# Queries and keys of a recurrence by seven products, and the first two products of every pair of blocks inside the recurrence

## The chip, the cores and the metric

The kernel runs on one core of a Trainium2 chip. The metric is the time of one execution on the device in microseconds (us); lower is better. The core has a matrix engine (TensorE, PE in the profile), a vector engine (VectorE, DVE), an engine for activation functions (ScalarE, ACT), a general one (GpSimd, POOL) and one that issues most of the transfers (SyncE, SP). Each works through its own queue in order and waits for the others by semaphores. TensorE writes to eight banks (PSUM), from which DVE and ACT read.

## The reference, cut to what matters

One layer of an encoder over x (1024 tokens x 1024 features, float32). The input projection is one matrix product; its columns are cut into the parts that the kernel treats one by one:

```python
proj = x @ w_in[l]
(aq, ak, av, gq, gk, gv, gout, lr_f, lr_b, gate_a, gate_g) = jnp.split(proj, IN_SPLITS, axis=-1)
...
# dilated windowed attention on aq, ak, av: 12 heads in 3 groups, mixed to 4 heads x 64
...
la_f = log_sigmoid(lr_f @ w_lr_fwd + b_lr_fwd) / TAU      # decays, low rank 16; la_b likewise
o_gla = forward scan(gq, gk, gv, la_f) + backward scan(gq, gk, gv, la_b)   # 4 heads, chunks
o_gla = o_gla * lax.rsqrt(jnp.mean(jnp.square(o_gla), axis=-1, keepdims=True) + NORM_EPS)
y_gla = o_gla * gla_norm_g * silu(gout)
...
merged = sigmoid(gate_a) * (y_attn @ w_attn_branch) + sigmoid(gate_g) * (y_gla @ w_gla_branch)
x = layernorm(ALPHA * x + merged @ w_out)
ff = square(relu(x @ w_ff1 + b_ff1)) @ w_ff2 + b_ff2
x = layernorm(ALPHA * x + ff)
```

gq and gk are 256 columns each (4 heads x 64), gv 512, gout 512, the two gates 1024 each, aq, ak and av 768 each.

## The kernel before, in words

**Three matmuls for one.** Every float32 operand is split into a rounded part (hi) and the rest (lo), by `halve` (a copy on ACT, a subtraction on DVE, lines 153 and 154) or `load_w` (93 and 95). `mm3` (lines 102 to 104) then does hi x hi, hi x lo and lo x hi. So one product over a slice of 128 features is three matmuls. A block is 128 columns of the projection; its result is kept feature by token, 128 x 1024.

**Seven products for eight.** Two blocks together are a pair. Weights (128-column blocks, halves of K) and x (halves of K, halves of the tokens) form a 2 x 2 by 2 x 2 block product, which `proj` does with seven products instead of eight (Strassen and Winograd's form). Each product is 12 matmuls of 512 columns. x's blocks are B11, B12 (first half of K; first and second half of the tokens), B21 and B22; its sums are T1 = B12 - B11, T3 = B22 - B12, T2 = B22 - T1 and T4 = B21 - T2. The weights' sides are A11, A12, A22 and sums S1 to S4, made by `side` from raw weights. The products: m1 = A11 B11, m2 = A12 B21 (these two together are the plain result of block 0 on the first half of the tokens), m6 = S2 T2, m7 = S3 T3, m5 = S1 T1, m4 = A22 T4, m3 = S4 B22. A step is one product with, three steps ahead, the making of its side (`steps`).

**The stages.**

1. Start (lines 180 to 206): x comes in slice by slice; the first blocks of queries and keys (blocks 0 and 2) are multiplied plainly, four banks, 96 matmuls. Constants and the bias rows follow.
2. `gla_v_units(0)`: eight units of 24 matmuls of 272 columns make low-rank rows and the first 240 columns of values. Values stay in the tile `gv`, queries and keys in tiles `q0` ... `k3`. The low-rank rows are transposed (`lrt`, lines 319 to 325).
3. The recurrence (`gla_head`, four heads). A head runs `pre1` (decays: the matmul `zp`, exponentials, logarithm, two scans on DVE), `pre2` (factors; keys are multiplied by `ex`, queries by `zb`), `turn` (transposes of keys), `intra`, `kv`, `states`, `out` and `outt`. Its steps depend on one another, so between them stand fills: eight units of values, four units that multiply blocks 1 and 3 plainly (24 matmuls each), and 14 fills of two halves each: the first two products (m1, m2) of the ten pairs in `KEPT`, and a part of the attention's values. Two units come before head 0's `pre1`, six between its `pre2` and its `turn`. `step` ties what it wraps to the last matmul issued, so TensorE runs this stage strictly in the order written.
4. x's sums (`xsum`, line 530, from x loaded once more) are made at the recurrence's end: T1 beside head 3, T3, T2 and T4 behind it.
5. `proj` for 16 pairs (`todo`): two of the swish gate, six of attention queries and keys, eight of the merge gates. Ten need five products only, the others seven. Between steps stand the attention's 24 tiles, eight per group: `visit` (scores, softmax, transposes, values) at set distances, 2 steps, then 1.75, and for the last nine visits what is left of the steps, 25 steps over nine visits. The last group's tiles also mix the three groups (lines 931 to 940, 955 to 971) and send weights through DRAM (`spread`, `loadw`). `silu` multiplies the recurrence's result by the swish gate and stores it.
6. `branches` loads both mixers' results and halves them; then the merge, the output projection and the MLP.

The order on each engine is set when the program is built: what is ready first by a planner's reckoning goes first, in order of the text, unless `issue_after` ties it behind a given instruction on the same engine. Pools are stacks at both ends of the memory; a pool with `reuse_waits="tile"` lets each of its tiles wait only for those tiles whose memory it takes. In a pool tiles lie in the order of their first mention.

Of the kernel before, what the change touches and what calls it, by code (L numbers as in the profile page):

```python
# [72 lines left out]
def build(tc, io):  # L73
# [32 lines left out]
    def mmtile(w=512):  # L106
# [4 lines left out]
    ygdr = dr.tile([4, 128, S], F32, name="ygdr")  # L111
# [9 lines left out]
    upk = dr.tile([10, 128, 512], F32, name="upk")  # L121
# [5 lines left out]
    XQ = {f"B{i + 1}{j + 1}": xp.tile([128, 2, 4, 512], F32R, tag="act", name=f"x{i}{j}")  # L127
          for i in range(2) for j in range(2)}
# [8 lines left out]
    def xl(k, sl):  # L137
        return xpart(1, k, sl)

    tbp = P.open("tbl", side="right")  # L140


    stp = P.open("start")
    w0 = {nm: (wp.tile([128, KT, 128], F32R, tag="whi", bufs=4, name="whi"),
               wp.tile([128, KT, 128], F32R, tag="wlo", bufs=4, name="wlo")) for nm in "qk"}

    def fetch(src, shape, tag, bufs, eng=SP):
        raw = stp.tile(shape, F32, tag=tag, bufs=bufs, name=tag)
        eng.dma_start(raw, src)
        return raw  # L150
# [4 lines left out]

    def start_w(k, n):
        if k:
            raw = fetch(io["wqk"][:, k:k + n], [128, n, 2, 128], f"w{n}", n)
        for i, nm in enumerate("qk"):
            hi, lo = w0[nm]  # L160
            r = raw[:, :, i] if k else fetch(io["wqk"][:, 0:1, i], [128, 1, 128], "w0", 2)
            halve(hi[:, k:k + n], lo[:, k:k + n], r, None if k else V.tensor_copy)

    def start_x(k, hf=None):

        sl = slice(0, S) if hf is None else slice(hf * 512, hf * 512 + 512)
        first = (k, hf) == (0, 0)
        raw = fetch(io["xT"][k * 128:(k + 1) * 128, sl], [128, S if hf is None else 512],
                    "xr" if hf is None else "xrh", 5 if hf is None else 4, A if first else SP)
        for j in range(2) if hf is None else (hf,):  # L170
            js = slice(j * 512, j * 512 + 512)
            r, h = raw[:, js] if hf is None else raw, xh(k, js)
            if first:
                V.tensor_copy(h[:, 256:512], r[:, 256:512])
                A.copy(h[:, 0:256], r[:, 0:256])
                V.tensor_tensor(xl(k, js), r, h.bitcast(F32), op=OP.subtract)
            else:
                halve(h, xl(k, js), r)


    zt = stp.tile([128, 512], BF16, name="zt")
    V.memset(zt, 0.0)
    zp = avp.tile([128, 512], F32, tag="av", name="zp")
    for _ in range(7):
        T.matmul(zp, zt[:, 0:128], zt, start=True, stop=True)

    ps0 = {("q", 0): mmtile(), ("q", 1): mmtile(), ("k", 0): mmtile(),
           ("k", 1): scp.tile([128, 512], F32, tag="sc", name="sc")}
    for k in range(KT):
        n = {0: 1, 1: 1, 2: 2, 4: 2, 6: 2}.get(k)  # L190
        if k == 0:
            start_x(0, 0)
        if n:
            start_w(k, n)
        if k == 0:
            start_x(0, 1)
        elif k < 3:
            start_x(k, 0)
            start_x(k, 1)
        else:  # L200
            start_x(k)
        for nm, hf in (("q", 0), ("k", 0), ("q", 1), ("k", 1)):
            hi, lo = w0[nm]
            sl = slice(hf * 512, hf * 512 + 512)
            mm3(ps0[nm, hf], [(hi[:, k], lo[:, k], xh(k, sl), xl(k, sl))],
                first=k == 0, last=k == KT - 1)


    ident = cp.tile([128, 128], F32, name="ident")
    SP.dma_start(ident, io["c_ident"])  # L210
    sgt = cp.tile([128, 128], F32, name="sgt")
    SP.dma_start(sgt, io["c_sgt"])
    cols = cp.tile([128, 56], F32, name="cols")
    SP.dma_start(cols, io["cols"])
    mhalf = cp.tile([128, 8], F32, name="mhalf")
    V.memset(mhalf, -0.5)

    rb = tbp.tile([99, 12], F32, name="rb")
    SP.dma_start(rb, io["rb"])
    oh = tbp.tile([99, 512], F32, name="oh")  # L220
    SP.dma_start(oh, io["c_oh"])
    tp = trp.tile([128, 512], F32, tag="tr", name="tr")
    T.matmul(tp[0:12], rb, oh, start=True, stop=True)
    tsb = tbp.tile([12, 512], F32, name="tsb")

    V.tensor_scalar(tsb, tp[0:12], 8.0, None, op0=OP.mult)
    SP.dma_start(trow, tsb)
    P.close("start")
    P.close("tbl")
    stg = P.open("stg", bufs=2, side="right")  # L230
    tmp = P.open("tmp", side="right")
    xr_t, xb_t = ring(tmp, [128, S], F32, 4, "xraw"), ring(tmp, [128, 512], F32, 3, "xb22")

    kp4 = P.open("keep", reuse_waits="tile")

    def piece4(name, dtype=F32, shape=(128, S), parts=128):
        return kp4.tile([parts, *shape[1:]], dtype, tag="k4", bufs=10, name=name)

    gp = P.open("gla", reuse_waits="tile")
    lr = gp.tile([128, 8, 3, 32], F32, name="lr")
    wz = gp.tile([96, 4, 128], F32, name="wz")

# [72 lines left out]
    for u in gv_units[1]:  # L317
        u()
# [1668 lines left out]
```

## Time and profile before

| what | value |
|---|---|
| median of 3 runs | 1362.0 us (1361.73 to 1362.38) |
| profiled execution, its own time | 1362.74 us |
| its span, from the first to the last instruction | 1360.9 us |
| mean granted TensorE clock | 0.998 |
| start until the last of the first 96 matmuls | to 29.9 us |
| values' first eight units and the recurrence | about 30 to 220 us |
| projections with attention | about 220 to 579 us |
| merge, output projection, MLP | from 579 us |

Rows of the profile are read so. A row of the timeline is start, duration, engine, line, operation, output <- inputs, shape, and how many; in square brackets stands how long the engine had been idle and what it waited for. A row of a window is its bounds and length, then for PE, PEld (weight loads), DVE, ACT and POOL the busy time and the number of instructions, then the granted clock, the transfers' share and GB/s. A row of groups is line, engine, operation, shapes and count, then busy time and mean ns of one, then idle time before them. A row of waits is who waited for whom: us in total, times, longest.

### The profile page before, as it was taken

The numbers are of one execution on the slowest core, as the hardware profiler recorded it, in microseconds if no ns is written. First come the engines' busy times: TensorE is split into PE (matmuls) and PEld (weight loads), VectorE is DVE, ScalarE is ACT, GpSimd is POOL, SyncE is SP. The second block draws the span as 40 slices with busy tenths as digits, with TensorE's granted clock in tenths as the row PEclk, the third lists the DMA queues.
The fourth block names the chain that finished last, engine by engine and source line by source line (L and its number), as shares of the span: only waits on it lengthen the run. The fifth ranks groups of instructions, "written<-read, shape, count | busy, mean of one in ns | idle before, by whom it ended". The sixth has DMA issues, their size and how long they took to land.

```text
span 1360.9 us, 18993 instructions
## 1 busy us (share of the span) xinstructions
PE 1349.8 (99%) x6781; PEld 1121.9 (82%) x6781; DVE 1025.2 (75%) x1764; ACT 630.9 (46%) x1199; POOL 122.6 (9%) x193
## 2 busy tenths in 40 slices
PE   9999999999999999999999999999999999999998
PEld 7988898898777777788888888888888888888886
DVE  6377669778776788767677777887767997786987
ACT  5346656323344444454337545555556433333343
POOL 0000001111443432000000000000000000000001
PEclk9999999999999999999999999999999999999999
DMA  7315754777656677666836466666736955444313
GB/s 250 81 46 177 246 170 144 263 256 220 187 193 217 175 212 198 201 200 235 291 143 230 139 216 201 226 200 203 267 149 193 364 193 165 145 154 155 93 32 124
DMA packets 126306, 256.96 MB, mean 189 GB/s; under 512 B 36053, under 2 KB 45877, under 8 KB 126212
## 3 DMA queue, kind: packets, MB, share of 16 engines
q1 hardware_dynamic: 117044, 229.55, 51.2%
q0 software_dynamic: 8736, 25.77, 6.2%
q8 instruction: 53, 0.87, 0.3%
q10 hardware_dynamic: 432, 0.44, 0.1%
q14 instruction: 41, 0.34, 0.1%
HBM read 175.61 MB, written 81.14 MB: 189 GB/s over the span
## 4 chain that ended last, share of the span: by engine, by line
PE 92%; DMA 3%; DVE 2%; ACT 2%; SPq 1%; issue 1%; ACTq 0%; DVEq 0%
PE ps L102 18%; PE ps L103 18%; PE ps L104 18%; PE mm L102 9%; PE mm L104 9%; PE mm L103 9%; PE avp L910 1%; PE sc L871 1%; PE tr L895 1%; DMA xrh<-in_xT 1%; ACT xr L1378 1%; PE sc L104 1%; PE sc L102 1%; PE sc L103 1%; DMA pwhi<-in_wtv 0%
## 5 line engine op out<-in xcount | busy, mean ns | idle before, releaser
L1359 ACT CAST T<-hp 128x1024 fp32r<-128x1024 f32 x36 | 37.9, 1052 | 109.0 <-PE ps L103 69.5
L103 PE MATMUL ps<-B,B 128*128 128x512 f32 x160 | 62.2, 389 | 0.0
L104 PE MATMUL ps<-B,B 128*128 128x512 f32 x160 | 62.2, 389 | 0.0
L1865 POOL TENSOR_TENSOR mv<-mv,mhalf 128x1 f32<-128x1 f32 x8 | 7.0, 881 | 607.3 <-DVE mv L1864 605.8
L102 PE MATMUL ps<-B,B 128*128 128x512 f32 x160 | 60.9, 390 | 0.5 <-ACT B L1359 0.5
L883 ACT ACTIVATE e<-e,sm 128x256 f32<-128x256 f32 (+2 forms) x96 | 43.3, 453 | 37.2 <-DVE sm L877 29.6
L102 PE MATMUL ps<-T,T 128*128 128x512 f32 x144 | 56.0, 389 | 0.0
L103 PE MATMUL ps<-T,T 128*128 128x512 f32 x144 | 56.0, 389 | 0.0
L104 PE MATMUL ps<-T,T 128*128 128x512 f32 x144 | 56.0, 389 | 0.0
L102 PE MATMUL ps<-B,T 128*128 128x512 f32 x144 | 56.0, 389 | 0.0
L103 PE MATMUL ps<-B,T 128*128 128x512 f32 x144 | 56.0, 389 | 0.0
L104 PE MATMUL ps<-B,T 128*128 128x512 f32 x144 | 56.0, 389 | 0.0
L1760 DVE TENSOR_TENSOR acc<-ps,acc 128x512 f32<-128x512 f32 x68 | 45.6, 685 | 12.7 <-PE ps L104 12.2
L1360 DVE TENSOR_TENSOR T<-hp,T 128x1024 fp32r<-128x1024 f32 x36 | 43.9, 1221 | 14.8 <-ACT T L1359 14.7
L102 PE MATMUL mm<-x,whi 128*128 128x512 f32 x136 | 53.4, 404 | 1.0 <-ACT x L153 0.6
L103 PE MATMUL mm<-x,whi 128*128 128x512 f32 x136 | 53.7, 395 | 0.0
L104 PE MATMUL mm<-x,wlo 128*128 128x512 f32 x136 | 53.5, 395 | 0.0
L102 PE MATMUL ps<-T,fraw 128*128 128x512 f32 x128 | 49.6, 390 | 0.4 <-ACT T L1359 0.4
L103 PE MATMUL ps<-T,fraw 128*128 128x512 f32 x128 | 49.8, 389 | 0.0
L104 PE MATMUL ps<-T,fraw 128*128 128x512 f32 x128 | 49.6, 389 | 0.0
L633 DVE TENSOR_TENSOR cr<-cu,mm 128x512 f32<-128x512 f32 x44 | 35.2, 799 | 19.2 <-PE mm L104 18.8
L1478 ACT ACTIVATE c<-c,cols 128x512 f32<-128x512 f32 x48 | 34.7, 725 | 30.2 <-DVE c L1539 13.7
(595 smaller groups left out, 4279.9 us busy)
## 6 DMA issues: line engine op xcount, KB each, us to landing
hdr<-c SPq DMA_DIRECT2D x112, 256.0 KB
hp<-hdr SPq DMA_DIRECT2D x56, 512.0 KB
spill<-cr SPq DMA_DIRECT2D x54, 256.0 KB
praw<-in_wfm SPq DMA_DIRECT2D x16, 512.0 KB
pwhi<-in_wfm SPq DMA_DIRECT2D x16, 512.0 KB
gate<-spill SPq DMA_DIRECT2D x32, 256.0 KB
wa<-in_w SPq DMA_DIRECT2D x16, 512.0 KB
wb<-in_w SPq DMA_DIRECT2D x16, 512.0 KB
```

The costliest lines, as they stand in the source:

```text
L102: T.matmul(ps, lh, rh, start=first and i == 0, stop=False, skip_group_check=more)
L103: T.matmul(ps, lh, rl, start=False, stop=False, skip_group_check=more)
L104: issued["pe"] = T.matmul(ps, ll, rh, start=False, stop=last and i == n - 1, skip_group_check=more)
L633: issued["add"] = V.tensor_tensor(o, a, b, op=OP.add)
L871: mm = T.matmul(sps[i][:, pr, 0:w], q[ps_, pr], k[ps_, pr, 0:w], start=True, stop=True)
L883: issued["exp"] = A.activation(e, e, AF.Exp, bias=sm[:, h:h + 1], scale=-1.0, accum_out=sm[:, 4 + h:5 + h])
L895: T.transpose(tp[0:hi - lo, pr, j], b["e"][i][:, pr, lo:hi], ident)
L910: return T.matmul(av[64 * i:64 * i + 64, pr], vv[:, h * 64:h * 64 + 64], b["et"][i][p0:p0 + vv.shape[0], pr, j], start=j == pr == 0, stop= ...
L1359: A.copy(o[:, 0], src)
L1360: V.tensor_tensor(o[:, 1], src, o[:, 0].bitcast(F32), op=OP.subtract)
L1478: A.activation(q, src, AF.Relu, bias=cols[:, 2 * j + f:2 * j + f + 1])
L1760: V.tensor_tensor(m, p, m, op=OP.add)
```

## The change

- **The start** holds x's first half of tokens only. Per slice of K it multiplies the query blocks 0 and 1 (m1 and m2 of two pairs: block 0 with 2, and 1 with 3), with a copy of m1 after four slices, and the first four value units' first group. Then come value units and, beside them, x's second half and the sums T1, T3, T2; T4 is written over B12, after B21 has been loaded again. B22 and T4 are stored to DRAM (`xsd`).
- **Queries and keys** of both pairs then take the other five products each (`psteps`). Results go to DRAM (`spill`) and come back as `q`, `k` per head (`load_qk`); values go through DRAM too (`gvd`) into `gv`. Head 0's `pre1` stands behind the first of the ten products, its `pre2` and `turn` behind the last.
- **Fills** are 20 in place of 26: m1 and m2 of all 16 pairs and the four values parts. No units of values, queries or keys are left there.
- **Projections** then need five products for each of the 16 pairs; T4 and B22 come back from DRAM. There are 90 steps instead of 98; the last nine visits share 19 steps.
- `silu` halves its result into the tiles of B11 and B21 instead of storing it; `branches` only loads the attention's result, into T3's tile. Tiles and pools are laid out anew (`pa`, `tk`, `xr`, `tp2`).
- All products of `proj` are now tied behind the last matmul; before, only from step 10 on.

The core of the diff:

```diff
-            with behind("pe" if "fixed" in issued else "none"), behind("small"):
+            with behind("pe"), behind("small"):
...
+    for k in range(KT):
+        start_x(k, 0)
...
+        for i in range(2):
+            o = first_sides[2 * (k // 4) + i]
+            with behind("pe"):
+                mm3(pq[i], [(o[:, 0, ks], o[:, 1, ks], xh(k, h0), xl(k, h0))], k == 0, k in (3, 7), k > 3)
+        for t in range(4):
+            v_unit(t, 0, pv[t], (k,))
...
+    for t in range(4):
+        v_unit(t, 1, v_bank(t))
...
+    for k in range(4):
+        b11, b12, b22 = block(k, 0), block(k, 1), block(k + 4, 1)
+        sub(b11, b12, b11)
+        split_x("T1", k, b11)
...
+    for t in range(4, 8):
+        v_unit(t, 0, v_bank(t))
+    lp = [trp.tile([128, 512], F32, tag="tr", name="tr") for _ in range(2)]
+    for t in range(8):
+        with behind("pe"):
+            mm = T.transpose(lp[t // 4][0:96, t % 4 * 128:t % 4 * 128 + 128], lr[:, t].rearrange("p a b -> p (a b)"), ident)
...
+    for t in range(4, 8):
+        v_unit(t, 1, scp.tile([128, 272], F32, tag="sc", name="sc"))
...
+    SP.dma_start(xsd[0], XQ["B22"].bitcast(F32))
+    for k in range(4):
+        b21, b22 = block(k, 1), block(k + 4, 1)
+        sub(b22, b21, b22)
+        split_x("T4", k, b22)
+    for prep, _ in psteps[4:]:
+        prep()
...
+    P.close("xr")
+    kp4 = P.open("keep", reuse_waits="tile")
...
+    def load_qk(h):
+        b, i = h // 2, h % 2
+        for nm, base in (("q", 0), ("k", 2)):
+            qk[nm, h] = t = piece4(f"{nm}{h}")
+            for d in range(2):
+                after_raw(SP.dma_start, t[64 * d:64 * d + 64], spill[base + b, 64 * i:64 * i + 64])
...
-            ex = piece4("ex")
+            ex = gp.tile([128, S], F32, tag="ex", name="ex")
...
-    fill(2)
-    step(heads[0]["pre1"])
-    heads[0]["pre2"]()
-    fill(6)
+    for n, (_, do) in enumerate(psteps):
+        if n == 1:
+            step(heads[0]["pre1"])
+        for f in do:
+            f()
+        if n == 4:
+            issued["raw"] = issued["sp"]
+            for h in range(2):
+                load_qk(h)
...
+    SP.dma_start(xsd[1], XQ["T4"].bitcast(F32))
+    P.close("pa")
+    gp = P.open("gla", reuse_waits="tile")
+    heads[0]["pre2"]()
+    firsts[1][1]()
+    gv = gp.tile([128, 8, 512], F32, name="gv")
+    for i in range(2):
+        after_raw(SP.dma_start, gv[:, 4 * i:4 * i + 4], gvd[512 * i:512 * i + 512].rearrange("(t p) f -> p t f", p=128))
...
+    tp2 = P.open("tp2", reuse_waits="tile")
+    for i, nm in ((1, "T4"), (0, "B22")):
+        XQ[nm] = tp2.tile([128, 2, 4, 512], F32R, name=f"y{nm}")
+        after_raw(SP.dma_start, XQ[nm].bitcast(F32), xsd[i])
...
-                          i - 2 if 1 < i < 2 + KEPT else None))
+        projs.append(proj(bl, r, (lambda i=i: projs[i + 2]["raw"]()) if 1 < i < NP - 2 else None, banks_of[i > 1], i))
...
-    n1 = len(steps) - 7
+    n1 = len(steps) - 5
...
-    for i in range(8):
-        for n, f in zip((6 + 2 * i, 12 + 2 * i), silu(i // 2, i % 2)):
+        for n, f in zip((10 + 2 * i, 16 + 2 * i), silu(i // 2, i % 2)):
```

Pool `pa` holds, in this order, B22, B12 (later T4), `first_sides`, `lr`, `rb`, two copies of m1 and the staging ring `fcr`; `keep` holds eight slots of 4 KB (`k4`: `lrt`, `wz`, `q`, `k`, `zb`, `L`), `wzr` and a mask; `gla` begins with `sm`, `ex` and `gv`.

864 lines of the change are left out of this document (404 added, 460 removed).

## The prediction

> **What bounds the kernel now.** I read the page's busy times and its chain of waits first, then TensorE's waits, then its timeline for the time from one matmul's start to the next.
>
> ```profile
> span 1360.9 us, 18993 instructions
> PE 1349.8 (99%) x6781; PEld 1121.9 (82%) x6781; DVE 1025.2 (75%) x1764; ACT 630.9 (46%) x1199; POOL 122.6 (9%) x193
> ...
> PE 92%; DMA 3%; DVE 2%; ACT 2%; SPq 1%; issue 1%; ACTq 0%; DVEq 0%
> ...
> PE tr L102 <- DVE cr L633: 0.8, 1, 0.8
> PE sc L977 <- DVE sm L877: 0.7, 2, 0.5
> ```
>
> TensorE (PE) is the bound: 99% busy, 92% of the chain, and the longest waits inside the kernel are under a microsecond. So the change is worth the matmuls it removes less the holes it opens in PE's queue.
>
> A busy matmul reads 389 ns because matmuls overlap; what one costs is the distance between starts:
>
> ```profile
> 473.05 0.39 PE L104 MATMUL mm<-xT,pwlo 128*128 128x512 f32 x1
> ...
> 476.45 0.39 PE L104 MATMUL mm<-x,px 128*128 128x512 f32 x1
> ...
> 53.35 0.29 PE L102 MATMUL mm<-whi,x 128*128 128x272 f32 x1
> 53.73 0.29 PE L102 MATMUL mm<-whi,x 128*128 128x272 f32 x1
> ```
>
> Between the first two rows lie 15 steps: 3.40/15 = 0.2267 us for 512 columns, so a product (12 matmuls) takes 2.72 us and a fill of two halves 5.44. The last two are three matmuls apart: 0.127 us for 272 columns, 3.03 us for a unit of 24.
>
> **Term 1, the matmuls removed.** Before, blocks 0 to 3 (queries and keys) cost 4 blocks x 2 halves x 24 = 192 matmuls. After, two pairs of blocks cost 7 products x 12 each: 168. 24 x 0.2267 = **-5.44 us**. The other six pairs' first two products only move into the recurrence, 144 matmuls or 32.6 us; values, gates and attention keep their counts.
>
> **Term 2, the start.**
>
> ```profile
> 4.26 1.19 PE L102 MATMUL mm<-x,whi 128*128 128x512 f32 x2
> 5.67 0.63 PE L104 MATMUL mm<-x,wlo 128*128 128x512 f32 x1
> 6.10 0.63 PE L103 MATMUL mm<-x,whi 128*128 128x512 f32 x1
> ...
> 14.65 0.50 PE L102 MATMUL mm<-x,whi 128*128 128x512 f32 x1 [0.58 <-ACT x L153]
> 25.16 1.03 PE L223 MATMUL tr<-oh,rb 99*12 99x512 f32 x2
> 29.67 0.39 PE L104 MATMUL sc<-x,wlo 128*128 128x512 f32 x1
> 0.00:20.00 20.00, 18.24 (x65) 12.65 (x66) 12.44 (x27) 11.85 (x23) 1.73 (x9) 1.00 0.82 289
> ```
>
> From 4.26 to 29.9 us PE ran 96 matmuls (21.8 us) and the bias rows (1.0): 2.9 us lost, partly to spacings of 0.43 us at first, partly waiting for x. After, one slice of K brings half as much x (256 KB), 128 KB of weights and 139 KB of value weights, and holds 6 x 0.2267 + 12 x 0.127 = 2.9 us of work: 523 KB per 2.9 us is 180 GB/s, against the 289 GB/s of the window row. Only six of the 512-column matmuls fall into the slow beginning (6 x 0.2 = 1.2 us lost, not waiting on x). I take **-1.45**, bounds 0 and -2.9.
>
> **Term 3, transposes of the low-rank rows.** They now stand in strict order behind value unit 7, whose copy by VectorE (DVE) the last one needs; before, a later unit covered it. Seven transposes run meanwhile. **+0.4**, bounds 0 and 1.
>
> **Term 4, the decays' first matmul.** Call F the end of the last value unit. PE reaches head 0's first matmul (`zp`, in `pre1`) at F + 0.5 (bias rows) + 2.72 = F + 3.2, the second at F + 3.45. Everything on PE is queued behind it. It needs `lrt` and `wzr`, whose memory in `keep` is the closed pool `xr`'s: the x blocks from which T4 is made, and pair 1's raw weights. T4 is written over B12, whose first slice of K the last value unit reads until F - 2.65 (7 of its 8 slices, 0.38 each, are left); ScalarE's first copy takes 0.6 more. So from about F - 1.9 DVE has 4 halves of T4, A22, S4, the bias rows, `wzr` (2) and `lrt` (4):
>
> ```profile
> 224.69 0.69 DVE L691 TENSOR_TENSOR praw<-praw 128x512 f32<-128x512 f32 x1
> 225.30 0.69 DVE L530 TENSOR_TENSOR xraw<-xraw 128x512 f32<-128x512 f32 x1
> 225.90 0.69 DVE L154 TENSOR_TENSOR pwhi<-psum,pwhi 128x512 fp32r<-128x512 f32 x1
> L306 DVE CAST wzr<-wz 96x512 fp32r<-96x512 f32 x1 | 0.4, 423 | 0.4 <-DMA wz<-in_wz 0.4
> ```
>
> Starts are 0.60 apart, so 12 x 0.60 + 0.4 = 7.6 us, done at F + 5.7: **+2.3**. Bounds: 0.5 if `lrt` goes first; 4.5 if the load of `wz` gets the slot of the bias table and starts only behind its matmul. Before, the same work lay among value units.
>
> **Term 5, head 0's keys.** The new code goes from the last product of queries and keys (end E) straight to `turn(0)` through `step`; before, six value units lay between. `turn` needs keys x `ex`, and `ex` now lies in pool `gla`. Tile sizes: const to `keep` end at byte 164,800 of a partition; `sm` takes 192, so `ex` is 164,992 to 169,088. `pa` is 62,528 long and, with the layout before ending at 229,344, begins at 166,816 with B22. B22 is read by that very last product (m3). So ScalarE's exponential cannot start before E:
>
> ```profile
> 73.96 1.06 ACT L360 ACTIVATE ex<-zb 128x1024 f32<-128x1024 f32 x1
> 75.05 1.22 DVE L361 TENSOR_TENSOR k<-k,ex 128x1024 f32<-128x1024 f32 x1 [1.58 <-ACT ex L360]
> ...
> 79.66 1.03 PE L371 MATMUL tr<-ident,k 128*128 128x128 f32 x8
> 80.63 1.16 PE L411 MATMUL sc<-q,k 64*128 64x128 f32 x16
> L364 DVE TENSOR_TENSOR q<-q,zb 128x1024 f32<-128x1024 f32 x4 | 4.9, 1231 | 2.0 <-ACT zb L363 1.9
> ```
>
> The last matmul's tail is 0.39 - 0.23 = 0.16; + 1.06 + 1.22 and some 0.1 for hand-overs = 2.6; then 0.2 before `intra`, whose queries are multiplied 1.2 later while the transposes take 1.03: **+2.8**. Upper bound 5.9, if `ex` must also wait for the last store from `fcr` (0.6 addition and a landing of 2.6, row below). Lower bound 2.6. `gv` is loaded over B22 and T4, so 2 x 1 MB start at E too: at 289 GB/s the second half lands at E + 7.3 + 2.6 = 9.9; `kv(1)` comes at E + 2.8 + 1.0 + 1.2 + 5.4 + 0.9 = 11.3. **+0.2**, upper bound 2.4 at the page's mean of 189 GB/s.
>
> **Term 6, the last attention tiles.** The last nine visits were spread over 25 products, now over 19: two products per visit instead of 2.78. Before shows one such visit, between these rows:
>
> ```profile
> 503.02 0.42 DVE L877 CUSTOM_DVE_ANT_0 e<-sc,strip 128x256 f32<-128x256 f32 x1
> ...
> 511.70 0.42 DVE L877 CUSTOM_DVE_ANT_0 e<-sc,strip 128x256 f32<-128x256 f32 x1 [0.81 <-PE sc L871]
> ...
> 503.85 0.28 PE L977 MATMUL sc<-ident,f 128*12 128x128 f32 x1 [0.45 <-DVE sm L877]
> 512.53 0.27 PE L977 MATMUL sc<-ident,f 128*12 128x128 f32 x1
> ```
>
> 8.68 us, of which DVE waited 0.81 for the scores; four of DVE's operations belonged to products. A pair whose first two products are kept needs 14 operations (5 halvings, 4 sums, 5 additions) for 5 products, 5.6 per visit: 1.6 x 0.60 = 0.96 more. That uses up the 0.81 and leaves 0.15; eight visits: 1.2, and a little for the spread's wait (0.45 above): **+1.5**. Bounds: 0 (sides are made three products ahead) and 8 x 0.96 = 7.7 (the wait stays).
>
> **Term 7, before the merge.**
>
> ```profile
> L1141 SPq DMA_DIRECT2D pre<-yadr x4: 319/342/382, 563.0 to 568.0; - x4
> DMA to landing us min/median/max: 2.2/2.6/4.7
> ...
> 561.09 0.42 DVE L940 TENSOR_TENSOR mixed<-W 128x256 f32<-128x256 f32 x1
> ...
> L102 PE MATMUL ps<-ya,whi x32: 389/389/389, 578.9 to 632.6; 128*128 128x512 f32 x32
> ```
>
> From the last mixing to the merge there were 17.8 us; five products instead of seven leave 12.4. Store, load, two landings of 2.6 and the halvings need about 9: **+0.3**, bounds 0 and 3.
>
> **At nothing.** Block sums T1 to T3 on DVE and ScalarE lie beside 12 value units, 36 us; DVE needs some 27 there (24 operations for the sums, 8 for x, 7 for sides at 0.60, weights and low-rank rows 3.6), so 9 are to spare. B22 and T4 come back as 4 MB, 14.5 us at 289 GB/s, beside the last fills and six products (16 us) that don't use them; uncovered, they would cost those 14.5. The extra stores and loads (SP issues) sit in queues nobody on PE waits for but `gv`'s. Six splits of 1024 columns join the recurrence, but 32 operations on block sums leave it, and twelve halvings (A11, A12) leave the attention. The swish gate's eight halvings move up from before the merge to steps 16 to 30 (4.8 us), where the fullest stretch was
>
> ```profile
> 300.00:320.00 20.00, 19.97 (x88) 16.22 (x87) 16.84 (x24) 5.33 (x9) 2.91 (x5) 1.00 0.68 211
> ```
>
> DVE at 16.84 of 20 us, with PE hardly waiting: they fit in what is left over some 40 us.
>
> Sum: -5.44 - 1.45 + 0.4 + 2.3 + 2.8 + 0.2 + 1.5 + 0.3 = **+0.6**. The profiled execution took 1362.74 (span 1360.9), the median is 1362.0; so 1363.3 for such an execution, **1362.6** as a median. About 0.2%, 2.7 us, is what a measurement of this kernel can tell from no change.
>
> **Rivals.** *Cover holds*: DVE takes `lrt` early and the attention's backlog is absorbed; only terms 1, 2, 3 and 5 stand: -3.7, 1358.3. For it: no TensorE wait over 0.8 us before; against: those waits had units between.
>
> *DVE becomes the bound of the last visits* (slower): its wait for the scores stays in the queue's order, and each of eight visits grows by 0.96. It decides once a visit's DVE work passes 8.7 us. 7.7 in place of 1.5: 1368.8.
>
> *The clock falls after the hole of term 5.* In the tail, where PE waits much, the granted clock drops:
>
> ```profile
> 1352.00:1354.00 2.00, 2.00 (x3) 0.67 (x2) 1.93 (x7) 0.57 (x1) 0.62 (x1) 0.51 0.00 0
> ```
>
> Holes of 0.8 us left no such mark. If it comes, the price is that of the beginning: half speed from the first dummy matmul (1.2 us) to 7.3, 6.1 us, half of it lost: 3.0, so 1365.6.
> The Trainium skill (TensorE: Matmul & The Clock Gate, Part 1: The HAM clock gate) has PE fall to half rate after about one idle window of 3.4 us, and Part 4 does not count transposes as busy; by it hole and transposes, 3.8 us, would be enough, at an estimated 1.7 us. No row here shows a hole of that size.
>
> **Chances.** Forecast (within 0.2%) 0.40; cover holds 0.30, all faster; DVE bound 0.14; clock 0.10; a worse hole in term 4 or 5 (to 1365.7) 0.06. So faster 0.30, same 0.40, slower 0.30. Range 1357.0 to 1370.0: below it lies only a start with nothing lost, above it bounds that add up. The forecast's own range is 1359.3 to 1364.7.
>
> **What would show it.** PE waiting on ScalarE or DVE 2 to 4 us ahead of L371's successor (first transposes of keys), and 1 to 4 us ahead of the first `zp`; `ex`'s first exponential starting right behind the last product; DVE over 9.5 tenths in the last visits. No hole at the first transposes would refute term 5; PE waits there together above 8 us would make it slower.

## The result and the profile after

The changed kernel takes 1411.27 us in the median of four runs (1409.84 to 1413.13), the kernel before 1361.87 (1361.05 to 1362.38): a ratio of 1.0364, with a 95% interval of 1.0346 to 1.0382. The sum of the prediction said +0.6 us and 1362.6; the medians say +49.4. The profiled executions differ by 47.1 in span, and the rest of this text explains those 47.1.

First the page of the kernel after, its span and TensorE's busy time:

```profile
span 1408.0 us, 19086 instructions
...
PE 1355.5 (96%) x6757; PEld 1124.3 (80%) x6757; DVE 1032.8 (73%) x1778; ACT 632.9 (45%) x1199; POOL 117.8 (8%) x185
```

PE has 24 matmuls fewer (6781 before), as term 1 counted. Yet it is busy for 5.7 us more (1349.8 before) and idle for 41.4 more: 1408.0 - 1355.5 = 52.5, before 11.1. Were all matmuls as fast as before, PE would be busy for 5.4 less; so about 11.1 us went into matmuls that ran slowly. 41.4 - 5.4 + 11.1 = 47.1: two questions, then, why PE waits and why it is slow.

Who PE waited for (line waiting, line waited for, us in total, times, longest):

```profile
PE sc L964 <- DVE f L958: 12.6, 4, 6.7
PE tr L523 <- DVE k L513: 10.6, 1, 10.6
PE sc L488 <- DVE wzr L459: 7.2, 1, 7.2
PE mm L102 <- ACT pwlo L149: 4.5, 1, 4.5
PE mm L102 <- DVE fcr L153: 4.2, 1, 4.2
PE mm L102 <- ACT fcr L367: 2.2, 1, 2.2
PE sc L964 <- DVE sm L864: 1.6, 2, 0.9
```

These seven groups make 42.9 us, where before no wait inside the kernel passed 0.8. By windows (bounds, length, PE's busy time first, the granted clock third from the end) they lie in few places:

```profile
72.00:140.00 68.00, 45.85 (x195) 36.42 (x194) 30.06 (x38) 18.66 (x26) 0.48 (x3) 0.82 0.56 179
140.00:270.00 130.00, 130.00 (x769) 112.65 (x768) 85.21 (x117) 77.98 (x179) 10.41 (x16) 1.00 0.65 207
270.00:300.00 30.00, 25.05 (x112) 20.80 (x111) 14.47 (x22) 9.81 (x16) 0.00 (x0) 0.94 0.48 169
520.00:640.00 120.00, 105.60 (x599) 82.89 (x596) 87.32 (x271) 43.90 (x116) 27.56 (x43) 0.96 0.68 200
```

The ten products of queries and keys and head 0's first steps (72 to 140) lose 22 us in waits, the projections' start 5, the last attention visits 14; the recurrence itself loses nothing. For the start, head 0 and the projections' beginning the order of time reads as follows (start, duration, engine, line; in brackets how long the engine stood idle, and for whom; SPq is SP's queue of transfers):

```profile
31.05 0.39 PE L102 MATMUL mm<-whi,xB 128*128 128x272 f32 x1 [2.23 <-ACT fcr L367]
...
70.13 0.32 SPq L705 DMA_DIRECT2D xsd<-xB  x1
71.92 0.31 SPq L444 DMA_DIRECT2D trow<-xr  x1
77.11 0.33 SPq L457 DMA_DIRECT2D wz<-in_wz  x1
79.95 0.68 DVE L459 TENSOR_TENSOR wzr<-wz,wzr 32x512 fp32r<-32x512 f32 x1
80.78 1.19 PE L488 MATMUL sc<-lrt,wzr 96*128 96x512 f32 x2 [7.25 <-DVE wzr L459]
82.20 0.63 PE L103 MATMUL mm<-xT,fs 128*128 128x512 f32 x1
82.63 0.63 PE L104 MATMUL mm<-xT,fs 128*128 128x512 f32 x1
...
86.34 1.23 DVE L495 TENSOR_TENSOR zb<-zb,L 128x1024 f32<-128x1024 f32 x1 [2.62 <-ACT L L492]
87.67 2.28 DVE L497 TENSOR_TENSOR_SCAN L<-rmask,zb 64x1024 f32<-64x1024 bf16 x1
89.99 2.29 DVE L498 TENSOR_TENSOR_SCAN L<-rmask,zb 64x1024 f32<-64x1024 bf16 x1
92.31 0.69 DVE L153 TENSOR_TENSOR fcr<-fu,mm 128x512 f32<-128x512 f32 x1
93.05 0.80 PE L102 MATMUL mm<-xB,fs 128*128 128x512 f32 x1 [4.19 <-DVE fcr L153]
...
119.09 1.04 ACT L93 CAST whi<-raw 128x1024 fp32r<-128x1024 f32 x1 [9.55 <-DMA raw<-in_wfm]
123.72 1.06 ACT L512 ACTIVATE ex<-zb 128x1024 f32<-128x1024 f32 x1
126.09 1.97 PE L523 MATMUL tr<-ident,k 128*128 128x128 f32 x8 [10.55 <-DVE k L513]
...
278.65 0.50 PE L102 MATMUL mm<-xT,pwlo 128*128 128x512 f32 x1 [4.54 <-ACT pwlo L149]
```

In each case an engine that isn't the bound stands in its own order: something late is ahead of something that PE needs.

- At 31.05 the second value units want a bank whose copy (L367, at 30.42) stands on ACT behind casts of x.
- At 80.78 head 0's decays want `wz`. SP issues its load at 77.11 only: its place is that of the bias table, and the table's store (71.92) has to land first, behind the 2 MB store of T4 (70.13).
- At 93.05 the third product wants a bank that DVE empties at 92.31. Ahead of that addition stand a subtraction that waited for ACT's logarithm and two scans of 2.3 us.
- At 126.09 the transposes want keys x `ex`. The last product ended at 115.5; ACT stood idle for 9.55 us at the cast of a kept pair's weights that were still on their way; a second pair's follows, and the exponential comes behind both.
- At 278.65 the first side of the projections is late; the experiments below look for the reason.

The spacing of the matmuls behind these waits is 0.43 us (82.20, 82.63) instead of 0.2267: that is the slow part.

In the last visits PE waits for one small operation of 0.16 us, the last of the four that make a tile's shares (L955 to L958). In the longest of these waits DVE is without a pause:

```profile
545.87 0.42 DVE L918 TENSOR_TENSOR W<-avp,W 128x256 f32<-128x256 f32 x1 [2.82 <-DMA W<-fdr]
...
554.02 0.17 DVE L957 RECIPROCAL f<-f 128x4 f32<-128x4 f32 x1
...
554.42 0.69 DVE L150 TENSOR_TENSOR pwhi<-psum,pwhi 128x512 fp32r<-128x512 f32 x1
...
556.05 1.20 DVE L926 TENSOR_TENSOR W<-R,W 128x128 f32<-128x128 f32 x4
557.17 0.68 DVE L889 COPY et<-tr 128x512 f32<-128x512 f32 x1
557.77 0.16 DVE L958 TENSOR_TENSOR f<-f 128x12 f32<-128x12 f32 x1
557.98 0.38 PE L964 MATMUL sc<-ident,f 128*12 128x128 f32 x1 [6.67 <-DVE f L958]
```

Between the last two share operations (554.02 and 557.77) DVE does part of a product's side, the next tile's scores with their bias, the mixing of an earlier tile and a copy.

### The profile page after: what moved, and what is told of

Its sections match the earlier page's. It is cut to its first block, busy times and chain, and to the rows that moved or that the text cites. A ratio compares the mean times of both kernels' runs of the same rounds, so it can differ in the third digit from the quotient of the medians.

```text
span 1408.0 us, 19086 instructions
## 1 busy us (share of the span) xinstructions
PE 1355.5 (96%) x6757; PEld 1124.3 (80%) x6757; DVE 1032.8 (73%) x1778; ACT 632.9 (45%) x1199; POOL 117.8 (8%) x185
## 4 chain that ended last, share of the span: by engine, by line
PE 57%; DVE 2%; issue 1%; ACT 1%; DMA 1%; POOL 0%; DVEq 0%; POOLq 0%; ACTq 0%
PE ps L102 18%; PE ps L103 18%; PE ps L104 18%; PE mm L102 1%; PE mm L103 1%; PE mm L104 1%; DMA W<-fdr 1%; ACT xr L1358 1%; DMA fdr<-fT 0%; PE ps L1355 0%; DVE W L926 0%; PE avp L897 0%; PE ps L1866 0%; DVE e L864 0%; DVE cr L153 0%
## 5 line engine op out<-in xcount | busy, mean ns | idle before, releaser
L93 ACT CAST whi<-raw 128x1024 fp32r<-128x1024 f32 (+1 forms) x31 | 30.1, 971 | 48.4 <-DMA raw<-in_wfm 30.9
L102 PE MATMUL mm<-xB,whi 128*128 128x512 f32 x128 | 51.3, 401 | 0.0
L103 PE MATMUL mm<-xB,whi 128*128 128x512 f32 x128 | 50.0, 390 | 0.0
L104 PE MATMUL mm<-xB,wlo 128*128 128x512 f32 x128 | 49.9, 390 | 0.0
```

The costliest lines, as they stand in the source:

```text
L93: A.copy(hi, raw)
L102: T.matmul(ps, lh, rh, start=first and i == 0, stop=False, skip_group_check=more)
L103: T.matmul(ps, lh, rl, start=False, stop=False, skip_group_check=more)
L104: issued["pe"] = T.matmul(ps, ll, rh, start=False, stop=last and i == n - 1, skip_group_check=more)
```

## The experiments

Each starts from the changed kernel and is given by its span (1408.0 without an edit; 1357.1 to 1361.6 for the kernel before in the same sittings), or by its time where it ran several times. All but one compute the whole reference. Most ran once. Four executions of the changed kernel itself have spans of 1408.0 to 1411.3, so between single runs a difference of up to 3 us in span says nothing by itself; there the waits decide.

**One cause at a time, start and head 0.** The bias table is moved out of `wz`'s place:

```diff
-    oh, tsb = xr[0][0:99], xr[1][0:12]
+    oh, tsb = xr[0][0:99], lr.rearrange("p t a b -> p (t a b)")[0:12, 0:512]
```

> Against the changed kernel (span 1408.0), only the 12 rows of the bias table are put into the memory of `lr` instead of `xr[1]`, whose place `wz` takes. Theory: the 7.25 us before head 0's first `zp` (L488) are the load of `wz` waiting until the bias table's store has landed (issued at 71.92, `wz` issued at 77.11). Then `wz` is issued at about 71, the wait falls to 1 to 3 us, the seven matmuls behind it no longer stand 0.43 apart, and the span falls by 5 to 7. Rival (term 4 of the prediction): VectorE's row of work makes lrt and wzr late; then the wait stays above 4 and the span falls by 3 at most.

Span 1407.7. The wait shrinks from 7.25 to 5.64 only. In its timeline:

```profile
71.12 0.87 SPq L457 DMA_DIRECT2D wz<-in_wz  x1
...
78.00 0.42 DVE L458 CAST wzr<-wz 96x512 fp32r<-96x512 f32 x1 [2.65 <-DMA wz<-in_wz]
```

Issued 6 us earlier, it lands only 1.5 earlier: 6.9 us from issue to use, where it had taken 2.4 when issued at 77.11. It stood behind T4's 2 MB, which at the 289 GB/s of the prediction's row take 7.3. The Trainium skill (DMA: Bandwidth & Descriptors, section Queues, rings and completion order) has each transfer engine take a queue's descriptors in ring order; this trace agrees. Memory was one cause, the store ahead in the queue the other: in the run with head 0's whole order below, `wz` is issued at 71.33, ahead of T4's store, and DVE uses it at 74.88 without a wait.

The two scans go two products later (`pre1` split, the scans behind the third product's addition):

> Against the changed kernel, the subtraction and the two scans of head 0's decays stand behind the addition of the third product instead of ahead of the second product's. Theory: the 4.19 us before the fourth product (waiting on VectorE's addition L153) come from these three, behind which the additions queue while they wait for ScalarE's logarithm; the wait goes, and with it the 11 spacings of 0.43 behind it (2.2): the products end 6 to 7 us earlier. The span falls by as much, or by less if the first transposes stay tied to the load of the weights (landing at 119). Rival: the additions were late for another reason (banks, stores from the ring fcr): the wait stays above 2.

Span 1406.1. The wait of 4.19 is gone, so it was the scans'. One of 2.37 came at 109.64: there DVE's roundings of the first kept weights, waiting for ACT's casts, stand ahead of a product's addition. The transposes still wait 9.9, since the loads are no earlier.

ACT's casts of the third and fourth kept pair go behind `zb`'s exponential:

```diff
+                issued["ex"] = A.activation(zb, zb, AF.Exp, scale=1.0 / TAU)
...
+            with behind("ex" if p in (2, 3) else "none"):
+                st["w"] = fm_pairs(*load_w(None, [128, KT, 128], st["raw"]), 0)
```

> Against the changed kernel, ScalarE's splits of the third and fourth kept pair stand behind head 0's exponentials. Theory: the 10.55 us before the first transposes are ScalarE waiting for the weights of these pairs (landed at 119, casts at 119.09 and 120.34) ahead of `pre2`; without it the wait is the 2.6 to 3 us of term 5, 7.5 less. Up to 3 of it come back if `gv` (issued behind further weights) is then what keys wait for: span 4.5 to 8 lower. Rival: the exponential waits for something else that ends at 120 (B22's or T4's store): the wait stays near 10.

Span 1402.4, and the chain of term 5 stands alone:

```profile
116.53 1.06 ACT L512 ACTIVATE ex<-zb 128x1024 f32<-128x1024 f32 x1 [3.99 <-PE av L104]
...
118.90 1.09 PE L523 MATMUL tr<-ident,k 128*128 128x128 f32 x8 [2.41 <-DVE k L513]
```

2.41 against the 2.6 that the prediction worked out for just this chain.

**The projections' start: three candidates.** Head 3's last steps ahead of the last fill:

> Against the changed kernel, the last head's final transposes stand behind one fill after `out`, and the other two fills behind them. Theory: the 4.54 us and the two small waits at 278.65 to 280.4 (5.3 in all) are the first sides, queued on ScalarE behind the scaling L591 that waits for those transposes; with two fills left (8 us) as cover they go, span 4 to 5.5 lower. Rival: the sides are late because of the load of T4, B22 and weights (360 GB/s from 260 to 280): the wait stays above 3.

Span 1408.7, the wait 3.90: no. The reload of T4 and B22 behind the last fill's store:

> Against the changed kernel, T4 and B22 (4 MB) are loaded back only behind the last store of the fills. Theory: their load, issued at 258, holds up the small stores of the fills; ScalarE's copies wait for their ring of four buffers (3.9 us until a store landed, where the last head's transposes came early), and the first sides stand behind those copies. Then the 4.5 us ahead of the first products go to 1 or less, and the span falls by 4 to 5; T4, needed six products later, comes just in time (0 to 2 back). Rival: sides late for their own weights or for the order on ScalarE: 4 us stay.

Span 1408.0, the wait 4.6: no. Both at once:

> Against the changed kernel, both edits that alone changed nothing: the last head's transposes ahead of the last two fills, and T4 and B22 loaded back behind the last store of the fills. Theory: each of the two alone is enough to hold ScalarE until the last fill's end (the scaling L591 in one, the copies that wait for stores behind the 4 MB in the other), so only without both are the first sides made early: the 4.5 us go to 1 or less, span 4 to 5.5 lower. Rival: the sides wait for a third thing (their weights' load): 3 or more stay.

Span 1412.7, the wait 4.31: no. Then the sides' memory, with both of these moves kept: the first three sides, which lay where the attention values' weights are read by the last fill, get memory of their own and stand in the text ahead of the last two fills (of the edit, this part):

```diff
-    p_side = turns([wt[1][0], wt[1][1], wt[0][2], wt[1][2], wt[0][3], wt[1][3], px], 7)
+    early = [tq.tile([128, 2, 512], F32R, name=f"pe{i}") for i in range(2)] + [px]
+    p_side = lambda: early.pop(0) if early else more_sides()
...
+    for i in range(3):
+        steps[i + 3][0]()
```

> Against the changed kernel, the first three sides get memory that no fill reads (two tiles of their own and `px`), stand in the text ahead of the last two fills, and the last head's transposes and the reload stand as in the run with both covers. Theory (third cover): the sides' tiles are those of the attention values' weights, which the last fill reads to its end; with own memory and their place ahead of the last copies the 4.3 to 4.6 us ahead of the first products go to 1 or less, with the slow matmuls behind them: span 4 to 6.5 lower than 1408.0 (1412.7 in the run with both covers). Rival (their raw weights land late): 3 or more stay.

Span 1401.1, and PE doesn't wait there (the same 30 us, this kernel):

```profile
255.00:285.00 30.00, 30.00 (x174) 27.96 (x173) 13.00 (x20) 11.93 (x36) 3.26 (x4) 1.00 0.75 265
```

Own memory, place in the text and the two moves together remove the wait; the moves alone don't (4.31). Memory and place are not separated, and neither was run without the moves.

**The last visits.** W is read from a constant input, so the shares' way through DRAM is left out and the output is not the reference's:

```diff
-                    one = fdr[t, i:i + 1].rearrange("i r n -> i (r n)")
+                    one = io["xT"][2 * t + i:2 * t + i + 1, 0:768]
```

> Against the changed kernel, the shares W of the last eight tiles are read from a constant input instead of from the DRAM place that `spread` has just written (the shares' way through DRAM is left out; the work of every engine stays). Theory: in the last visits VectorE stands in order behind `mix`, which waits for W's way through DRAM (9.2 us in four waits, the longest 4.7), and TensorE then waits for `f` (12.6 us); without it TensorE's waits at the share transposes fall below 4 us in all and the span by 8 to 12. Rival (DVE's work alone, the prediction's slower case): a visit's work on VectorE exceeds the 9 us that a visit now has; then TensorE's waits there stay above 9 and the span falls by 4 at most.

Span 1409.5; the waits at L964 for `f` fall from 12.6 to 10.0. The round trip that DVE waits for (2.82 above) is the smaller part, and the span doesn't gain by it. The last visits further apart, the others closer:

```diff
-    at = [2 * min(i, 8) + 1.75 * min(max(i - 8, 0), 8) for i in range(26)]
+    at = [1.75 * min(i, 16) for i in range(26)]
...
-        n = n0 + 5 + int(at[i] + max(i - 16, 0) * (n1 - 6 - n0 - at[-1]) / 9)
+        n = n0 + 3 + int(at[i] + max(i - 16, 0) * (n1 - 4 - n0 - at[-1]) / 9)
```

> Against the changed kernel, the visits begin two steps earlier and the first sixteen stand 1.75 steps apart, so that the last nine have 2.56 products each instead of 2.11. If the last visits are what is too dense (by either theory), the waits at the share transposes fall from 14 us to 4 or less and the span by 9 to 13; if the wait is fixed per tile (the way through DRAM takes longer than a visit of any such length), they stay above 9.

Span 1420.9, 13 us worse, and a surprise: 2.56 steps per visit are gaps of two and three by turns, and PE waits at every second visit, 2.90, 4.82, 5.73 and 4.99. The shares one step sooner:

```diff
-        for k, part, later in ((i, 4, 1), (i, 5, 2), (i - 2, 9, 1), (i - 1, 7, 1)):
+        for k, part, later in ((i, 4, 1), (i, 5, 1), (i - 2, 9, 1), (i - 1, 7, 1)):
```

> Against the changed kernel, in the last eight tiles the shares (`f`, down to L958) are issued one step earlier, right behind the weights' exponential. Theory (order on VectorE): neither DVE's total work nor W's way through DRAM makes TensorE wait at the share transposes (with the way left out 10.0 us of 12.6 stayed, and with wider visits they grew to 18.4), but that the shares' last two operations stand on VectorE behind the operations of the next visit and the next sides wherever that visit comes two steps later and not three. One step earlier they are ahead of them: the waits fall from 14 us to 5 or less, the span by 8 to 14. Rival (work): 9 or more stay.

Span 1405.4: the waits at L964 fall from 14.2 (both groups) to 6.9, but 2.25 come at the merge's first matmul, which now waits for the attention's result. Less work for DVE (the copies of `et` on ACT, R x W in two operations instead of four):

> Against the changed kernel, in the last eight tiles VectorE does less: ScalarE copies all transposed weights (0.6 us a tile less on VectorE), and the four multiplications of R by W are two of twice the width (about 0.4 less): 1.0 of the 8.7 us that VectorE has for a visit. Theory (VectorE is the bound of the last visits, the prediction's slower case): each visit gets up to 1.0 shorter until TensorE's 8.75 sets it; the waits there fall from 14 us to 7 or less and the span by 6 to 12. Rival (order and transfers): the waits stay above 10 and the span falls by 3 at most.

Span 1406.6, the waits at L964 for `f` 10.9, the longest 4.7 in place of 6.7. DVE's amount of work alone is not it.

**Together.** For head 0, `wz` and the first kept weights load ahead of T4's store, `pre1` comes one product later, the scans behind the fifth product's addition (the text put on record says the fourth), the casts behind `ex`, one fill ahead of the transposes:

> Against the changed kernel: bias table in the memory of `lr`; the loads of `wz` and of the first two pairs' weights ahead of T4's store (2 MB, behind which `wz` landed 5.8 us after its issue even where the bias table was out of its way); head 0's `pre1` one product later and its scans behind the fourth product's addition; the third and fourth pair's splits behind the exponentials; one fill ahead of the first transposes. Theory: these four waits are all of the loss between 72 and 140; `zp` waits 0 to 1, no wait over 1 us on the additions, none at the transposes, and no half-rate matmuls: 20 to 24 us off the span (1384 to 1388). Rival: the waits are linked, and a further transfer (q and k, `gv`) takes their place with more than 5 us.

Span 1389.6: 18.4 back; of the 22 us in waits between 72 and 140, 2 are left (PE busy 65.86 of 68). To this, the second value units start in the free bank, the low-rank transposes come a unit later, head 0's `ex` takes `wz`'s place, `gv` is loaded by heads, and the fill ahead of the transposes goes; the two edits tried together for the sides, and the shares' earlier step, come along:

> Against the changed kernel, together: head 0's order as before in this study, but without the fill ahead of the transposes: `ex` of head 0 is put into the memory of `wz`, so that it does not wait for the last product, the scans stand behind the third product's addition, and `gv` is loaded head by head; both covers of the run beside this; the shares one step earlier; and at the start the free bank first (2.2 us) and the low-rank transposes a unit later (1.0). If the causes found are all, the sum is 23 + 2.4 + 4.5 + 10 + 3.2, some 43 us: span 1363 to 1370, about that of before (1360.9). If waits come back elsewhere, 1375 or more.

Span 1381.7. Up to 72 us PE is idle for 1.3 in place of 4.4, the transposes run at 97.76 instead of 126.09 and wait 1.74; the sides' wait (4.31) stays, and the last visits keep 7.2 us of waits at the shares. With the sides' own memory in place of the moved last fill, and DVE relieved by the two edits tried above:

> Against the run that put all causes together (span 1381.7): with the sides' own memory in place of the two covers, and with less on VectorE in the last visits. Theory: 5 from the first sides and 6 to 12 from the last visits: span 1365 to 1371. If both theories fall, 1378 to 1382.

Span 1371.1; what is left is 6.1 at the last shares and 3.2 ahead of the merge. Now the visits start sooner and stand 1.5 apart, which leaves the last nine 2.89 steps each, and one scan moves again:

> Against the run d3_together (span 1371.1): head 0's second scan behind the fourth product's addition, so that the last queries and keys are stored sooner (1.6 and 1.1 us at the first transposes and scores), and the visits spread anew: they begin two steps earlier, the first sixteen stand 1.5 steps apart (lighter on VectorE: no shares, no mixing), the last nine 2.89, and the last ends one step earlier. Theory (VectorE is the bound of the last visits at 2.1 products each, order decides the rest): the waits of the last visits and of the merge's beginning (11.7 us) fall to 4 or less and nothing comes up among the first sixteen: span 1360 to 1364. If spacing is not what sets them (as with 2.56 products, where it got worse), 1371 or more.

Span 1366.7. One wait of 3.21 is left at the shares, and it stands behind a gap of three steps; the only gap of two has none. The same with the old start and end, 2.78 steps for the last nine:

```diff
-        n = n0 + 3 + int(at[i] + max(i - 16, 0) * (n1 - 5 - n0 - at[-1]) / 9)
+        n = n0 + 5 + int(at[i] + max(i - 16, 0) * (n1 - 6 - n0 - at[-1]) / 9)
```

> As the run beside it, but the visits begin where the changed kernel begins them and end where it ends them: first sixteen 1.5 steps apart, last nine 2.78 (as before the change). If only the last nine's distance counts, 1361 to 1365; if the last store's way to the merge counts too (3.2 us at the first merge product), 2 to 3 more than the run beside it.

Span 1362.7. The gaps are now 2, 3, 3, 3, 2, 3, 3, 3, 3 steps, and the two larger waits are the two gaps of two:

```profile
475.40 0.28 PE L999 MATMUL sc<-ident,f 128*12 128x128 f32 x1 [2.08 <-DVE sm L900]
...
522.28 0.38 PE L999 MATMUL sc<-ident,f 128*12 128x128 f32 x1 [3.10 <-DVE sm L900]
```

So the visits stand 1.375 apart, which makes all the last gaps three, and a fill goes ahead of the transposes:

```diff
-    at = [1.5 * min(i, 16) for i in range(26)]
+    at = [1.375 * min(i, 16) for i in range(26)]
...
+    fill(1)
...
-        if h != 1:
+        if h > 1:
             fill(1)
```

> Against the run e2_last_three_late (1364.85, span 1362.7): the first sixteen visits 1.375 steps apart, so that each of the last nine has exactly three products (with 2.78 two of nine gaps were of two steps, and the two waits left, 2.1 and 3.1 us, stood at the visits behind them); and head 0's fill stands ahead of its first transposes instead of ahead of its keys x values (its transposes waited 2.7 us for the load of k). Theory: the two gaps cost 5 to 6 with the slow matmuls behind them, the transposes 1.5 to 2.5: 1356 to 1359, ratio to the kernel before 0.996 to 0.998. If a gap of three steps does not end the waits, or the first sixteen become too dense, 1362 or more.

1366.3 us (1365.92 to 1368.89) against 1360.91, a ratio of 1.0044 (1.0031 to 1.0058). The two waits are gone (1.9 in sum at the shares), but the fill's own copy stands in the way of head 0's queries:

```profile
106.70 0.59 ACT L625 COPY xb<-mm 128x512 f32<-128x512 f32 x1 [17.98 <-DMA gv<-gvd]
...
109.68 2.08 PE L578 MATMUL sc<-q,k 64*128 64x128 f32 x16 [7.77 <-DVE q L530]
```

Without that fill, all else the same:

> f1_last without the fill ahead of head 0's transposes, all else the same (attention units 1.375 steps apart, the last nine visits three steps apart). Theory (three things made the 49: queue order at the start and before the heads, the sides' memory read by the last fill, gaps of two steps among the last visits): the wait of 7.77 us for head 0's queries at 109.68 is gone, since no fill's copy stands ahead of zb's exponential; the first transposes wait again some 2.7 us for the loads of k and q (as in e2_last_three_late), the last visits keep losing under 2 us in waits. Span 1364.5 - 7.8 - 0.6 for slow matmuls + 3.1 = about 1359, a ratio to the kernel before of 0.997 to 1.000. Rival 1 (the last fills moved by the one fill less ahead of the turn collide with something later): the wait at the turn stays away but another of over 3 us comes between 110 and 310, 1362 or more. Rival 2 (the last visits were covered only because the earlier wait had let DVE run ahead): waits over 3 us after 480, 1364 or more.

1363.29 us (1361.65 to 1364.86) against 1361.42, a ratio of 1.0015 (1.0006 to 1.0024). Page and waits of an execution of 1362.39:

```profile
span 1360.5 us, 19090 instructions
...
PE 1345.2 (99%) x6757; PEld 1118.2 (82%) x6757; DVE 1027.1 (75%) x1753; ACT 635.1 (47%) x1208; POOL 117.9 (9%) x185
```

```profile
PE sc L999 <- DVE sm L900: 2.7, 3, 2.0
PE tr L537 <- DVE k L527: 2.4, 1, 2.4
```

No new wait of over 3 us came, which speaks against both rivals, though the median is some 2 us above what was expected. Together the edits bring back all but 2 of the 49; what each cause is worth by itself was not measured, and less work for DVE and `gv` by heads are among them. PE is busy for 4.6 us less than before, near term 1's 5.4, and idle for 15.3, 4.2 more. The time is about 0.15% above that of the kernel before, with an interval just above 1: inside the 0.2% that the prediction took for no change, but on its slower side. No version here beats the kernel before. One wait at the shares, 2.0 at 544, stays though all gaps are three steps: the gap isn't the whole of it.

Step by step, spans: 1408.0; head 0's order 1389.6; start, `ex`, `gv` and shares 1381.7; sides' memory and DVE's work 1371.1; visits' distances and one scan 1366.7 and 1362.7; gaps of three 1360.5.

## Why the prediction was wrong

| step | predicted | measured in the changed kernel |
|---|---|---|
| 1 matmuls | -5.44 | 24 fewer; PE's busy time -4.6 in the last kernel above |
| 2 start | -1.45 | -1.6 until 28.7, then a wait of 2.23 |
| 3 low-rank transposes | +0.4 | 1.02 |
| 4 first `zp` | +2.3 (0.5 to 4.5) | 7.25, and 1.4 of slow matmuls |
| scans ahead of the additions | not seen | 4.19, and 2.5 of slow matmuls |
| 5 first transposes | +2.8 (2.6 to 5.9) | 10.55, and 1.5 of slow ones |
| 6 last visits | +1.5 (0 to 7.7) | 14.2 of waits, and slow matmuls |
| 7 before the merge | +0.3 | none |
| first sides | at nothing | 4.54 and 0.42, and slow matmuls |

**Right**: what bounds the kernel, the worth of term 1, the start's first part (48 matmuls of 512 and 96 of 272 columns, 23.1 us, took 24.3; before, 2.9 were lost). Term 7 came out partly by luck: nothing waits there in the changed kernel, but once the last visits had lost less, 2.25 and 3.2 us appeared ahead of the merge, the second beyond the term's bound of 3. Of term 5 the mechanism was right, and with the casts out of the way its size too (2.41 for 2.6). The clock rival was right in its mechanism, but was put at 0.10 as an alternative, with 3.0 for one hole: slow matmuls came behind every long hole and cost about 11 in all.

**Term 4** failed in its bounds. The prediction saw that `wz` takes the bias table's slot, and let the load start behind the table's matmul. It starts behind the landing of the table's *store* (71.92 to 77.11), which stands behind T4's 2 MB. What stands ahead was asked for PE and DVE; SP's queue was put "at nothing". It also priced `pre1` on PE alone: that it puts two scans on DVE between a product and its addition was not looked at.

**Term 5** took ACT as free ("ScalarE's exponential cannot start before E"). The rows of before show the exponential with nothing ahead of it; in the new order two casts are, and they wait for loads.

**"At nothing"** failed for the first sides. The reload was priced (14.5 if uncovered) and is indeed covered, as moving it showed; but not the memory in which the sides are made, and who reads it last.

**Term 6** was mis-sized: 14.2 against +1.5, and past its upper bound of 7.7. Its sample visit (503.02 to 511.70) already was one of two steps, and PE doesn't wait behind it (512.53). But in the kernel before the gaps of the last visits were 2, 3, 3, 3, 2, 3, 3, 3 and 3 steps, so a short gap stood alone. In the changed kernel eight gaps of two follow one another, and the waits at their shares are 0.67, 0, 1.42, 6.67, 0, 0.95, 0.55 and 3.95. DVE isn't the bound by its sum of work, as the rival had it: from the first to the last of these shares (523.33 to 599.59) it is busy for 58.5 of 76.3 us, not over 9.5 tenths, and taking about 1 us of its work out of each visit brought 1.4 us of span. But the work is uneven: ahead of the wait of 6.67 DVE does 12.0 us of it between two shares (542.43 to 557.98), in which PE has 8.9, and the small share operations stand in DVE's order among it. What mostly covers this is a whole step's matmuls more per visit. Over the changed kernel and the five with other distances, PE waits at gaps of two 0 to 6.7 us, over 2 at eight of fifteen; at gaps of three it waits over 0.5 only three times in 33, but once 3.21. So the gap is most of the cause; that the uneven work is the rest is not shown, since no run evened it out.

The large errors have one sign, and most of them one root: the sum was made of work per engine, while an order written by hand was being replaced, and what stands in each order was only read for PE.

## What to carry to other kernels

When work between two dependent steps is taken away, list for every engine and every transfer queue what will stand ahead of the instruction that PE waits for, and when that can start; a DMA that is late for one thing holds everything behind it on that engine. Memory counts as an order too: a tile's first write waits for the last reader of its place, stores among them. And count covers in whole steps and for the fullest visit, not in averages.

## What the runs showed of the hardware

A hole in PE's work can cost more than its length, because the matmuls behind it run slowly. In the changed kernel those behind the holes of 4.19, 6.67 and 7.25 us start 0.43 us apart instead of 0.227, 12, 11 and 7 of them, and the granted clock is 0.55 (93 to 99), 0.60 (557 to 564) and 0.53 (80 to 85). The slow stretch, 4.0 to 5.3 us, doesn't grow with the hole.

Shorter holes go either way, and their length alone doesn't decide it. Behind one of 2.37 us in the kernel with the scans later

```profile
109.64 0.50 PE L102 MATMUL av<-xB,swlo 128*128 128x512 f32 x1 [2.37 <-DVE fcr L153]
...
110.22 0.39 PE L104 MATMUL av<-xB,swlo 128*128 128x512 f32 x1
...
111.11 0.63 PE L104 MATMUL av<-xB,swlo 128*128 128x512 f32 x1
111.53 0.63 PE L102 MATMUL av<-xB,swlo 128*128 128x512 f32 x1
```

four follow 0.23 to 0.34 apart and then seven at 0.43. The kernel with the shares one step sooner has slow matmuls at once behind 2.18 us, and none behind 3.16:

```profile
551.88 0.38 PE L964 MATMUL sc<-ident,f 128*12 128x128 f32 x1 [2.18 <-DVE sm L864]
...
552.49 0.63 PE L103 MATMUL mm<-yT,px 128*128 128x512 f32 x1
552.91 0.63 PE L104 MATMUL mm<-yT,px 128*128 128x512 f32 x1
...
574.16 0.27 PE L964 MATMUL sc<-ident,f 128*12 128x128 f32 x1 [3.16 <-DVE f L958]
...
574.50 0.40 PE L103 MATMUL mm<-xT,pwlo 128*128 128x512 f32 x1
574.74 0.39 PE L104 MATMUL mm<-xT,pwlo 128*128 128x512 f32 x1
```

The hole of 2.2 us at the start, near 31 us, stands in several kernels whose text ahead of it is the same. In the changed kernel the value matmuls behind it keep their 0.127 us, at a granted clock of 1.00 (31 to 40); with the scans later, with the casts behind `ex` and without the round trip a dozen or more of those that follow are 0.23 apart, at 0.81. So something that the kernel's text doesn't set decides as well; which it is stays open, and it is part of what single runs differ by.

The Trainium skill (TensorE: Matmul & The Clock Gate, Part 1: The HAM clock gate) has the clock halve after an idle window of about 3.4 us that runs free of the program; the halved rate agrees, and so does the loose phase, but here holes shorter than that, 2.18 and 2.37, were enough.
